# Near-attention scores issued among the last projection panels of a two-layer diffusion backbone

## The chip, the cores and the metric

The kernel runs on one core of one Trainium2 chip. It is one program: TensorE (PE, with its weight loads PEld), VectorE (DVE), ScalarE (ACT), GpSimd (POOL) and SyncE (SP, which mostly issues DMAs) each run a list of instructions in order, and semaphores make one list wait for another. The metric is the device time of the whole program in microseconds, as the median of several executions.

## The reference

The model is two transformer layers over 512 latent tokens (a grid 64 wide, 8 rows) and 256 context tokens, with a width of 1024. The change concerns the first layer's attention, and there the eight neighbourhood heads. Its core:

```python
def na_heads(q, k, v, qc, kc, vc, rel_bias, ctx_out):
    ...
    s_lat = jnp.einsum('bnqhd,bknmhd->bhnqkm', qr, k_blk).astype(jnp.float32) * scale
    s_lat = s_lat + col_bias[:, dr_idx].transpose(0, 2, 3, 1, 4)[None]
    s_lat = jnp.where(col_ok[:, :, None, :], s_lat, NEG_INF)...
    s_ctx = jnp.einsum('bnqhd,bchd->bhnqc', qr, kc).astype(jnp.float32) * scale
    p = jax.nn.softmax(jnp.concatenate([s_ctx, s_lat], axis=-1), axis=-1)
    return p_ctx @ vc + p_lat @ v_blk
    ...
def even_mixer(a_lat, a_ctx, ...):
    p_lat = a_lat @ w_in          # one projection for all head groups
    p_ctx = a_ctx @ w_in
    o_mla = mla_heads(...)
    o_na = na_heads(...)
    return concatenate([o_mla, o_na]) @ w_out
```

Each latent query sees the keys of 16 columns around it in all 8 rows, with a learned bias by distance, and all context keys, in one softmax. Context queries see the context keys alone. Behind the mixer comes a SwiGLU; the second layer has sliding-window attention.

## The kernel before

Everything is float32. A product of two float32 matrices is made of three matmuls of a high and a low part (`mm3`, lines 345, 347 and 348). Activations lie with features on the partitions and 768 tokens along the row: 512 latent ones and 256 context ones.

**The projection panels.** `projections()` walks over twelve panels of the input projection. A panel loads 128 output features of the weight, splits it, and makes two runs of 24 matmuls, 512 columns wide for the latent tokens and 256 for the context ones (`project`). It yields after every two of the eight steps over the width, so a panel has eight yields and the whole loop 96. The last four panels are the queries and keys of the third and fourth pair of near heads. Between the yields `bg` starts pieces of the conditioning vectors (`mod_tile`): products on VectorE (L239), products on GpSimd (L256) whose sums ScalarE makes (L257), and small sums on VectorE (L243, L259, L260).

**The near heads.** When the panels are through, `attend(na_jobs())` runs. Near heads come in four pairs. A pair has three jobs: context query tiles 4 and 5, latent query tiles 0 and 1, latent query tiles 2 and 3, each job for both heads of the pair. A job has a front half: for each query tile, scores on TensorE into one of three PSUM banks called `s` (`stacked_scores`, L755 and L756), then `take` on VectorE (L565), which adds the bias tile and the negated score and takes the row's minimum, then the exponential with its sum on ScalarE (L561). Its back half transposes the probabilities on TensorE (L509), copies them out of PSUM on VectorE or ScalarE (L500, L501), and multiplies them with the values (L555). `attend` keeps one job's lag: it works on a job's front and on the back of the one before in turns given by `PATTERN`, with side work (`step`) mixed in.

**Side work of the near heads.** `split_pair` makes the high and low parts of the third and fourth pair's queries (`put_q`, L721 and L722) and keys (`put_k`, L735 and L736); for the third pair the high part of the keys is cast on VectorE, and the halves are then copied across partitions by four DMAs. `latent_norms` normalizes the compressed latents (sums of squares L995, root L998, reciprocal L999, gains L975). `mix` copies values for mixed tiles on GpSimd (L1143).

**The bias tiles.** A head has two bias tiles of 128 x 768 (384 KB), one for query tiles 0 and 1, one for 2 and 3. All of them share two buffers, tag `nb`. `nb_tiles(h)` is called for one head at a time and issues both of its loads, so the buffers are taken in the order head 0 first half, head 0 second half, head 1 first half, head 1 second half.

**What sets the order.** The program is traced in the order in which Python runs it, and each instruction has a priority from its place there, which `shifted` moves. The scheduler then places the instructions on each engine by priority and by when their inputs are ready in its own timeline. `behind(a, b)` fixes that a comes after b on the same engine.

Of the kernel before, what the change touches and what calls it, by code (L numbers as in the profile page):

```python
# [2 lines left out]

# [9 lines left out]
ALU = mybir.AluOpType  # L13

P = 128
# [4 lines left out]
NT = NL + NX  # L20
# [9 lines left out]
LOWEST = -3.0e38  # L30
# [27 lines left out]
KC = (0, 1, 0)  # L58
# [12 lines left out]
LATE = ((0, 1, 3, 5, 7), ()), (0,) * 4 + (1, 2, 2, 2, 1, 2, 2, 2, 1, 2, 3, 2, 1, 2, 3, 2, 0, 0), ((2,), (2,)) + ((0, 2, 4, 6),) * 3  # L71
FIRST = 2000
STEPS = ((2, 3, 4, 4), 5, 3)
HALVES = (slice(0, 256), slice(256, 512))
# [25 lines left out]
def hybrid_kernel(ctx: ExitStack, tc, I, out):  # L100
# [33 lines left out]
    def dma(o, i, eng=None):  # L134
        return (eng or nc.sync).dma_start(f(o), f(i))
# [182 lines left out]
    def bg(n=1):  # L318

        for _ in range(n):  # L320
            next(mods, None)
# [241 lines left out]
    def take(p, c, s, bias, start, nm):  # L563

        V.tensor_tensor_reduce(out=p[:, c], in0=s, in1=bias, op0=ALU.add, op1=ALU.min, scale=-1.0, scalar=start,  # L565
                               accum_out=nm)

# [160 lines left out]

    def put_k(ks, copies=True, hi=None):


        def use(src, c):
            for side, (k1, k2) in enumerate(ks):
                r, x = slice(64 * side, 64 * side + 64), slice(64 - 64 * side, 128 - 64 * side)
                (hi or S.copy)(k1[r, c], src[r])  # L735
                V.tensor_tensor(k2[r, c], src[r], f(k1[r, c]), op=ALU.subtract)  # L736
# [293 lines left out]
    def split_pair(p):  # L1030
# [6 lines left out]
        yield  # L1037
        put_k(sets[p][1], KC[1], how[RK[p - 2]])(k, slice(0, NT))
        yield
# [94 lines left out]
    VX = []  # L1134
# [10 lines left out]
    def na_jobs():  # L1145
        for p in range(4):
# [8 lines left out]
            sums, mins = T("sm", [P, 6, 2]), T("sm", [P, 6, 2])  # L1155
            hs = []
            for s in range(2):
                t1, ks = sets[p]
                hs.append(Head(s, stacked_scores(t1[s], ks[s]), keys_of(VN[p], s, VX[p]), None, nb_tiles(2 * p + s), -LOWEST, sums, mins))
            yield from pair_jobs(hs, po, True, finish(po, sums, 6))  # L1160
# [656 lines left out]
```

## Time and profile before

| | us |
|---|---|
| median of three executions | 1577.79 (1577.0 to 1583.72) |
| the profiled execution | 1578.6 |
| its span, first to last instruction | 1576.6 |
| TensorE busy in it | 1530.6 |
| VectorE busy | 1174.0 |
| ScalarE busy | 794.5 |
| GpSimd busy | 276.0 |

The span in forty equal slices, each digit the busy share of a slice in tenths, and the TensorE clock that was granted:

```profile
PE   6999999999999999999999999999999999999998
PEld 4787778887998999999999998877889999899998
DVE  4885777685878587777858675889976778678685
ACT  4563677775465243242423334548856545454453
PEclk9999999999999999999999999999999999999999
```

One slice is 39.4 us. The panels end in the fifth, and the near heads fill the rest of it and the sixth and seventh. A row of a timeline gives start and duration in us, engine, line, operation, output and inputs by the program's names, shapes, and in brackets how long the engine sat idle before it and what ended that. A row of the busy view gives a stretch, its length, then the busy time of TensorE, its weight loads, VectorE, ScalarE and GpSimd with their instruction counts, the granted clock (1.00 is full), the share of the DMA engines and their rate.

### The profile page before, as it was taken

The numbers are of one execution on the slowest core, as the hardware profiler recorded it, in microseconds if no ns is written. First come the engines' busy times: TensorE is split into PE (matmuls) and PEld (weight loads), VectorE is DVE, ScalarE is ACT, GpSimd is POOL, SyncE is SP. The second block draws the span as 40 slices with busy tenths as digits, with TensorE's granted clock in tenths as the row PEclk, the third lists the DMA queues.
The fourth block names the chain that finished last, engine by engine and source line by source line (L and its number), as shares of the span: only waits on it lengthen the run. The fifth ranks groups of instructions, "written<-read, shape, count | busy, mean of one in ns | idle before, by whom it ended". The sixth has DMA issues, their size and how long they took to land.

```text
span 1576.6 us, 26539 instructions
## 1 busy us (share of the span) xinstructions
PE 1530.6 (97%) x10024; PEld 1375.8 (87%) x10024; DVE 1174.0 (74%) x2345; ACT 794.5 (50%) x1607; POOL 276.0 (18%) x302
## 2 busy tenths in 40 slices
PE   6999999999999999999999999999999999999998
PEld 4787778887998999999999998877889999899998
DVE  4885777685878587777858675889976778678685
ACT  4563677775465243242423334548856545454453
POOL 0144624320111101102111131470012000000001
PEclk9999999999999999999999999999999999999999
DMA  9644242004654444646466494110125123323222
GB/s 317 250 131 175 78 129 73 11 7 160 207 168 143 154 165 161 219 134 264 157 202 236 146 351 145 49 46 2 68 78 164 52 98 126 98 90 128 86 96 87
DMA packets 76463, 214.90 MB, mean 136 GB/s; under 512 B 9872, under 2 KB 16400, under 8 KB 76336
## 3 DMA queue, kind: packets, MB, share of 16 engines
q1 hardware_dynamic: 59216, 144.42, 27.6%
q0 software_dynamic: 15968, 67.24, 12.3%
q8 instruction: 78, 1.28, 0.3%
q10 hardware_dynamic: 1152, 1.57, 0.3%
q14 instruction: 49, 0.40, 0.1%
HBM read 186.97 MB, written 23.07 MB: 133 GB/s over the span
## 4 chain that ended last, share of the span: by engine, by line
PE 79%; DVE 9%; DMA 5%; ACT 3%; issue 2%; POOL 1%; SPq 0%; DVEq 0%; ACTq 0%; POOLq 0%
PE pss L1388 5%; PE pss L1387 5%; PE pss L1386 5%; PE pso L555 4%; PE pss L345 4%; PE psd L345 4%; PE pss L348 4%; PE pss L347 4%; PE psd L348 4%; PE psd L347 4%; PE pst L345 3%; PE pst L1388 3%; PE pst L1386 3%; PE pst L348 3%; PE pst L347 3%; PE pst L1387 3%
## 5 line engine op out<-in xcount | busy, mean ns | idle before, releaser
L334 ACT CAST wh<-wr 128x1024 fp32r<-128x1024 f32 (+2 forms) x148 | 115.5, 795 | 210.9 <-DMA wr<-in_w_dn_dram 42.1
L335 DVE TENSOR_TENSOR wl<-wr,wh 128x1024 fp32r<-128x1024 f32 (+2 forms) x145 | 133.9, 930 | 81.7 <-ACT wh L334 81.5
L561 ACT ACTIVATE p<-p,sm 128x512 f32<-128x512 f32 (+3 forms) x144 | 105.0, 730 | 29.0 <-DVE sm L565 27.2
L1386 PE MATMUL pss<-b,wh 128*128 128x384 f32 (+1 forms) x346 | 107.8, 312 | 0.6 <-ACT b L371 0.6
L1387 PE MATMUL pss<-b,wh 128*128 128x384 f32 (+1 forms) x346 | 108.0, 312 | 0.1
L1388 PE MATMUL pss<-b,wl 128*128 128x384 f32 (+1 forms) x346 | 107.2, 312 | 0.0
L347 PE MATMUL psd<-b,wh 128*128 128x512 f32 (+3 forms) x262 | 89.7, 343 | 0.0
L301 DVE CUSTOM_DVE_ANT_0 p<-rope,cond 128x1024 bf16<-128x1024 f32 x64 | 76.9, 1221 | 11.0 <-DMA rope<-in_mod_w_dram 10.8
L291 POOL DMA_DIRECT2D rope<-in_mod_w_dram x48 | 25.6, 533 | 318.7 <-DVE mod L301 306.0
L345 PE MATMUL psd<-b,wh 128*128 128x512 f32 (+3 forms) x222 | 80.0, 360 | 1.2 <-ACT b L474 0.9
L348 PE MATMUL psd<-b,wl 128*128 128x512 f32 (+3 forms) x222 | 78.8, 356 | 0.0
L555 PE MATMUL pso<-ph,b 128*64 128x256 f32 (+1 forms) x384 | 77.5, 361 | 0.4 <-DVE ph L500 0.2
L555 PE MATMUL pso<-pl,b 128*64 128x256 f32 (+1 forms) x384 | 77.2, 359 | 0.0
L1386 PE MATMUL pst<-b,wh 128*128 128x384 f32 (+1 forms) x226 | 70.8, 313 | 3.1 <-ACT p L1436 1.8
L1373 ACT CAST wh<-pl 128x512 fp32r<-128x512 f32 x78 | 44.9, 619 | 52.0 <-PE pss L1387 22.8
L1388 PE MATMUL pst<-b,wl 128*128 128x384 f32 (+1 forms) x226 | 70.7, 313 | 0.2 <-DVE wl L1374 0.2
L1387 PE MATMUL pst<-b,wh 128*128 128x384 f32 (+1 forms) x226 | 70.6, 312 | 0.0
L347 PE MATMUL pss<-b,wh 128*128 128x256 f32 (+3 forms) x216 | 69.3, 321 | 0.0
L1373 ACT CAST wh<-wr 128x1024 fp32r<-128x1024 f32 x39 | 41.0, 1051 | 54.4 <-PE pst L1387 14.7
L345 PE MATMUL pss<-st,wh 128*128 128x512 f32 (+2 forms) x198 | 67.2, 339 | 0.3 <-ACT wh L334 0.3
L348 PE MATMUL pss<-st,wl 128*128 128x512 f32 (+2 forms) x198 | 67.3, 340 | 0.1
L1386 PEld LDWEIGHTS pss<-b,wh 128*128 128x128 f32 x346 | 65.7, 190 | 1.1 <-ACT b L371 0.9
(624 smaller groups left out, 5387.4 us busy)
## 6 DMA issues: line engine op xcount, KB each, us to landing
wr<-in_w_gu_dram SPq DMA_DIRECT2D x88, 512.0 KB, 4.1
rope<-in_mod_w_dram POOLq DMA_DIRECT2D x48, 512.0 KB, 3.9
wr<-in_w_dn_dram SPq DMA_DIRECT2D x73, 256.0 KB, 2.9
wr<-in_w_out_dram SPq DMA_DIRECT2D x32, 512.0 KB, 4.2
p<-home POOLq DMA_DIRECT2D x40, 384.0 KB, 5.5
home<-p POOLq DMA_DIRECT2D x40, 384.0 KB, 5.4
wr<-in_w_in_dram SPq DMA_DIRECT2D x21, 512.0 KB, 3.8
nb<-in_nb_dram SPq DMA_DIRECT2D x16, 384.0 KB, 3.3
```

Of the source, the lines that this page charges most:

```text
L301: behind(V.tensor_tensor_reduce(out=T("p", [P, D], mybir.dt.bfloat16), in0=w, in1=cond[:, v, :], op0=ALU.mult, op1=ALU.add, scale=1.0, sca ...
L334: behind(S.copy(h, r), *after[:1])
L335: behind((G if eng else V).tensor_tensor(lo, r, f(h), op=ALU.subtract), *after[1:])
L345: ins = PE.matmul(o, wh[:, k], mh[:, c], start=first and k == 0, stop=False)
L347: PE.matmul(o, wh[:, k], ml[:, c], start=False, stop=False)
L348: PE.matmul(o, wl[:, k], mh[:, c], start=False, stop=last and k == n - 1)
L555: ins = PE.matmul(o[64 * i : 64 * i + 64, c], v(kt), t, start=n == 0, stop=n == len(moving[i]) - 1)
L561: S.activation(p[:, c], p[:, c], AF.Exp, bias=nm, scale=-1.0, accum_out=dn)
L1373: S.copy(h, t)
L1386: PE.matmul(o, wh, xh, start=first and k == 0, stop=False, skip_group_check=not first)
L1387: PE.matmul(o, wh, xl, start=False, stop=False, skip_group_check=not first)
L1388: PE.matmul(o, wl, xh, start=False, stop=k == 3, skip_group_check=not first)
```

## The change

It has three parts.

- `fronts()` takes the first two jobs of `na_jobs()` and runs their front halves (scores, `take`, exponentials) from inside the projection loop: a piece at each of the yields 82, 84, 86, 88, 90, 92 and 94, that is in the last two panels. `attend` then gets these jobs with an empty first step (`resumed`), and the others as before. What stands ahead of the first `yield` in `na_jobs` (the first side work, `mix`, the bias loads, `split_pair`'s start) is thereby traced earlier too.
- `nb_tiles(p)` is called for a pair, and issues the first halves of both heads, then the second halves.
- For the third pair, `split_pair` waits two more steps between queries and keys, and its first cast of the keys must stand behind the latest `take` that has been traced by then (`marks["take"]`).

```diff
+FRONTS = (82, 84, 86, 88, 90, 92, 94)
+QUIET = 2
...
-        V.tensor_tensor_reduce(out=p[:, c], in0=s, in1=bias, op0=ALU.add, op1=ALU.min, scale=-1.0, scalar=start,
-                               accum_out=nm)
+        marks["take"] = V.tensor_tensor_reduce(out=p[:, c], in0=s, in1=bias, op0=ALU.add, op1=ALU.min, scale=-1.0, scalar=start,
+                                               accum_out=nm)
...
-    def put_k(ks, copies=True, hi=None):
+    def put_k(ks, copies=True, hi=None, after=()):
...
-                (hi or S.copy)(k1[r, c], src[r])
+                behind((hi or S.copy)(k1[r, c], src[r]), *after)
...
-    def nb_tiles(h):
-        ts = [T("nb", [P, NT]) for i in range(2)]
+    def nb_tiles(p):
+        ts = {}
         for i in range(2):
-            dma(ts[i], I["nb"][h, i])
+            for s in range(2):
+                ts[s, i] = T("nb", [P, NT])
+                dma(ts[s, i], I["nb"][2 * p + s, i])
         cut = (slice(0, 512), slice(256, 768), slice(256, 768), slice(0, 512))
-        return lambda n: ts[n // 2][:, cut[n]]
+        return [lambda n, s=s: ts[s, n // 2][:, cut[n]] for s in range(2)]
...
-        put_k(sets[p][1], KC[1], how[RK[p - 2]])(k, slice(0, NT))
+        if p == 2:
+            for _ in range(QUIET):
+                yield
+        put_k(sets[p][1], KC[1], how[RK[p - 2]], after=(marks["take"],) if p == 2 else ())(k, slice(0, NT))
...
-    i = 0
+    def resumed(j):
+        yield False
+        yield from j
+
+    def fronts():
+        for _ in range(2):
+            early.append(next(jobs))
+            yield from iter(early[-1].__next__, False)
+
+    jobs, early, i = na_jobs(), [], 0
+    ahead = fronts()
     for _ in projections():
         i += 1
         bg(int(i * DBG) - int(i * DBG - DBG))
+        if i in FRONTS:
+            next(ahead, None)
+    for _ in ahead:
+        pass
     dense[0] = False
-    attend(na_jobs())
+    attend(chain((resumed(j) for j in early), jobs))
```

The lines of the changed file stand three to five further down: the scores L755 and L756 are L758 and L759 there, `take` L565 is L568, the transposes L509 are L512, the key split L735 and L736 is L738 and L739, DMAs of L135 are of L138.

What that does to the order is shown at three places. The first is TensorE at the end of the last panel. Before, the last two products of the panel's context run (`pst_1773`) are followed by the first context scores of both heads:

```order
L347 MATMUL pst_1773<-b_113,wh_1735 128x256
L348 MATMUL pst_1773<-b_112,wl_1736 128x256
L755 MATMUL pss_1833<-st_654,st_652 128x256
L756 MATMUL pss_1833<-st_655,st_652 128x256
L755 MATMUL pss_1843<-st_656,st_653 128x256
L756 MATMUL pss_1843<-st_657,st_653 128x256
```

In the changed kernel a near tile of the second head (`pss_1834`) stands between the latent run (`psd_1793`) and the context run of the same panel, and behind that run come the transposes of the first job:

```order
L350 MATMUL psd_1793<-b_113,wh_1789 128x512
L351 MATMUL psd_1793<-b_112,wl_1790 128x512
L758 MATMUL pss_1834<-st_656,st_653 128x192
L759 MATMUL pss_1834<-st_657,st_653 128x192
L758 MATMUL pss_1834<-st_656,st_653 128x64
L759 MATMUL pss_1834<-st_657,st_653 128x64
L758 MATMUL pss_1834<-st_656,st_653 128x256
L759 MATMUL pss_1834<-st_657,st_653 128x256
L348 MATMUL pst_1845<-b_98,wh_1789 128x256
...
L351 MATMUL pst_1845<-b_112,wl_1790 128x256
L512 MATMUL pst_1899<-ident_r_86,p_1693 128x128 x4
L512 MATMUL psd_1906<-ident_r_86,p_1715 128x128 x4
```

So the scores of the first two jobs, 28 matmuls, all stand ahead of the panel's end; the last of them are those shown.

The second place is VectorE, where the third pair's key split stood. Before, it lies among the last products of the conditioning and ahead of the first `take`; `b_1855` to `b_1857` are parts of the third pair's keys, `pl_1784` a conditioning weight:

```order
L735 CAST b_1855<-p_1563 64x768
L239 ISA p_1786,mod_293_1376<-pl_1784,cond_66,mod_293_1376 128x512
L239 ISA mod_293_1376 128x1
L736 TENSOR_TENSOR b_1856<-p_1563,b_1855 64x768
L735 CAST b_1857<-p_1563 64x768
L243 SCALAR_TENSOR_TENSOR mod_293_1376<-mod_293_1376,modb_89 128x1
L565 ISA p_1834,sm_1824<-pss_1833,zeros_95 128x256
```

In the changed kernel the same parts are `b_1891` to `b_1893`, and they stand among the takes of the first pair's last job (bias tile `nb_1690`), the fourth pair's key split (`st_2164`), and the second pair's first takes:

```order
L738 CAST b_1891<-p_1563 64x768
L739 TENSOR_TENSOR st_2164<-p_1786,st_2163 64x768
L568 ISA p_1994,sm_1683<-pss_1991,nb_1690 128x512
L568 ISA sm_1683 128x1
L568 ISA p_2009,sm_1999<-pss_2008,zeros_95 128x256
L568 ISA sm_1999 128x1
L503 COPY ph_1968<-pst_1963 128x512
L739 TENSOR_TENSOR b_1892<-p_1563,b_1891 64x768
L738 CAST b_1893<-p_1563 64x768
L568 ISA p_2033,sm_1999<-pss_2032,zeros_95 128x256
```

The split has moved from ahead of the near heads to behind the takes of two jobs and part of a third.

The third place is the queue of SyncE. The first two bias tiles are loaded long before in both programs. Before, the next ones are both halves of the first pair's second head (`nb_1829`, `nb_1830`), then the second pair's first head (`nb_2000`, `nb_2001`), with the copies of the third pair's keys (`b`) ahead of them:

```order
L135 DMA b_1855<-b_1855 64x768
L135 DMA b_1856<-b_1856 64x768
L135 DMA b_1857<-b_1857 64x768
L135 DMA b_1858<-b_1858 64x768
L135 DMA nb_1829<-in_nb_dram 128x768
L135 DMA nb_1830<-in_nb_dram 128x768
L135 DMA nb_2000<-in_nb_dram 128x768
L135 DMA st_2163<-st_2163 64x768
L135 DMA nb_2001<-in_nb_dram 128x768
```

In the changed kernel they are the second halves of both heads of the first pair (`nb_1688`, `nb_1690`), then the first halves of both heads of the second (`nb_2000`, `nb_2002`), with the key copies between and behind them:

```order
L138 DMA nb_1688<-in_nb_dram 128x768
L138 DMA nb_1690<-in_nb_dram 128x768
L138 DMA st_2163<-st_2163 64x768
L138 DMA nb_2000<-in_nb_dram 128x768
L138 DMA b_1891<-b_1891 64x768
L138 DMA st_2164<-st_2164 64x768
L138 DMA nb_2002<-in_nb_dram 128x768
L138 DMA st_2165<-st_2165 64x768
L138 DMA b_1892<-b_1892 64x768
L138 DMA b_1893<-b_1893 64x768
```

The bias loads keep their number and size; each is now issued when a first half has been used by its head, and the key copies stand behind two bias loads.

More of the change, by code (lines that the diff above doesn't have):

```diff
@@ L2 @@
 from contextlib import ExitStack, contextmanager
+from itertools import chain
 import numpy as np
@@ L1155, in na_jobs @@
             sums, mins = T("sm", [P, 6, 2]), T("sm", [P, 6, 2])
-            hs = []
+            hs, near = [], nb_tiles(p)
             for s in range(2):
                 t1, ks = sets[p]
-                hs.append(Head(s, stacked_scores(t1[s], ks[s]), keys_of(VN[p], s, VX[p]), None, nb_tiles(2 * p + s), -LOWEST, sums, mins))
+                hs.append(Head(s, stacked_scores(t1[s], ks[s]), keys_of(VN[p], s, VX[p]), None, near[s], -LOWEST, sums, mins))
             yield from pair_jobs(hs, po, True, finish(po, sums, 6))
```

## The prediction

> **What bounds the kernel now.** I read the page first, then the busy time by stretches around the place of the change, then the timelines of TensorE, VectorE and ScalarE inside those stretches, and last the answer on the bias tile.
>
> ```profile
> PE 1530.6 (97%) x10024; PEld 1375.8 (87%) x10024; DVE 1174.0 (74%) x2345; ACT 794.5 (50%) x1607; POOL 276.0 (18%) x302
> ```
>
> TensorE is busy for 1530.6 of 1576.6 us, so all that any change of order can win is in the other 46.0 us, and in stretches at a lower clock. The next view says where some of both lie: the last projection panels, then the near heads up to the last bias step of the second pair (211.02), then the rest of the near heads, then the heads behind them.
>
> ```profile
> core 0: us, PE busy (x) PEld busy (x) DVE busy (x) ACT busy (x) POOL busy (x), PEclk, DMA share, GB/s
> 159.15:175.83 16.68, 16.68 (x98) 14.77 (x97) 12.44 (x25) 7.52 (x18) 10.81 (x9) 1.00 0.04 14
> 175.83:211.02 35.19, 31.29 (x222) 26.18 (x220) 25.14 (x70) 27.88 (x66) 15.95 (x11) 0.90 0.46 128
> 197.50:211.02 13.52, 13.10 (x112) 11.61 (x110) 10.88 (x29) 11.16 (x25) 0.00 (x0) 1.00 0.53 146
> 211.02:257.40 46.38, 43.76 (x316) 35.09 (x315) 37.80 (x89) 35.22 (x85) 19.16 (x15) 0.96 0.31 94
> 257.40:355.00 97.60, 96.99 (x729) 78.92 (x729) 69.25 (x203) 72.09 (x165) 28.89 (x20) 1.00 0.09 24
> ```
>
> In the panels TensorE has no idle time (16.68 of 16.68), while ScalarE is busy for only 7.52 us. Behind them it idles for 35.19 - 31.29 = 3.90 us, and then for 2.62 us. From 257.40 on it is busy for 99%, so whatever arrives there earlier stays earlier. The clock column is 0.90 and 0.96; a finer grid shows why.
>
> ```profile
> 176.22:179.64 3.42, 2.24 (x13) 1.40 (x11) 3.33 (x8) 3.19 (x8) 3.22 (x4) 1.00 0.56 136
> 179.64:183.05 3.41, 3.00 (x14) 3.00 (x15) 1.75 (x8) 2.37 (x7) 3.25 (x3) 0.50 0.27 58
> 183.05:186.47 3.42, 3.42 (x17) 3.42 (x18) 0.25 (x1) 0.85 (x4) 3.34 (x3) 0.50 0.37 115
> 189.88:193.29 3.41, 1.99 (x14) 1.46 (x12) 0.96 (x3) 3.36 (x8) 2.84 (x2) 1.00 0.74 214
> 210.36:213.77 3.41, 1.57 (x9) 1.19 (x10) 3.41 (x9) 2.51 (x6) 0.65 (x1) 1.00 0.78 214
> 213.77:217.19 3.42, 3.42 (x15) 2.12 (x15) 2.93 (x8) 3.42 (x8) 3.34 (x4) 0.50 0.14 49
> ```
>
> Three stretches run at half clock, each set right behind a stretch in which TensorE was busy for 2.24 us or less (183.05 follows another slow one). That is 10.25 us at half speed, or 5.1 us of lost work. While TensorE crawls, VectorE is busy for 0.25 of 3.42 us: it waits for TensorE, not the other way round.
>
> ```profile
> 175.71 0.28 PE L348 MATMUL pst<-b,wl 128*128 128x256 f32 x1
> 180.05 0.53 PE L755 MATMUL pss<-st,st 128*128 128x192 f32 x1 [0.84 <-DVE sm L565]
> 193.50 0.39 PE L755 MATMUL pss<-st,st 128*128 128x256 f32 x1 [1.62 <-DVE sm L565]
> 213.44 0.79 PE L509 MATMUL psd<-ident_r,p 128*128 128x128 f32 x4 [1.54 <-DVE b L975]
> 186.22 0.69 DVE L500 COPY pl<-pst 128x512 f32<-128x512 f32 x1 [3.78 <-PE pst L509]
> 192.74 0.69 DVE L565 CUSTOM_DVE_ANT_0 wr<-pss,nb 128x512 f32<-128x512 f32 x1 [2.45 <-DMA nb<-in_nb_dram]
>   DVE wr L565: 3.5, 3
> DMA to landing us min/median/max: 2.9/3.1/4.0
> ```
>
> The first row is the last projection product. The next three are TensorE's waits: twice for a score bank that L565 on VectorE (add the bias, take the minimum) must empty. The last three rows say that this step itself waits 3.5 us in all for bias tiles, since of the four tiles of a pair the third is loaded only when a buffer comes free, with a landing time of about 3.1 us. So the stage is a **chain of latencies**: scores, L565, exponential, transposes, copies, with each engine between 71% and 89% busy.
>
> **The change, part by part.** Durations are those of the profiled execution, 1578.6 us long with a span of 1576.6; that is 0.8 us above the median of the runs, 1577.79, and I subtract that at the end.
>
> *Scores moved ahead.* The new order puts the scores of two jobs between the projection products: four context tiles and the first near query tile of both heads, sixteen matmuls 256 columns wide, and the second near query tile of both heads, two groups of six.
>
> ```profile
> 176.07 0.28 PE L755 MATMUL pss<-st,st 128*128 128x256 f32 x1
> 176.19 0.28 PE L756 MATMUL pss<-st,st 128*128 128x256 f32 x1
> 203.09 0.25 PE L755 MATMUL pss<-st,st 128*128 128x192 f32 x1
> 203.77 0.49 PE L509 MATMUL pst<-ident_r,p 128*128 128x128 f32 x3
> 164.82 1.14 DVE L260 SCALAR_TENSOR_TENSOR mod<-mod,modb 128x1 f32<-128x1 f32 x1
> ```
>
> Wide ones follow each other by 0.12 us: 16 x 0.12 = 1.9. A group of six runs from 203.09 to 203.77: 2 x 0.68 = 1.4. TensorE issues in order, so a score that needs a bank again stops the panel until L565 has run. The first L565 stands behind the L260 that ends here at 165.96, and with 0.34 of its own and the read of the sum it ends about 166.4; TensorE is back at that bank after 12 products of 0.23, 8 of 0.12 and two scores from 162.0, at about 165.9. I put 0.4 us down for it; the bounds are 0 and the 6 us of the slow rival below. The panels then end at 175.83 + 1.9 + 1.4 + 0.4 = **179.5**. Nothing of this is won yet: the same matmuls are missing behind it.
>
> *Work behind the panels.* What was between 175.83 and 211.02 is now this, for VectorE and ScalarE:
>
> ```profile
> 177.03 0.41 DVE L565 CUSTOM_DVE_ANT_0 p<-pss,zeros 128x256 f32<-128x256 f32 x1
> 177.37 0.41 DVE L565 CUSTOM_DVE_ANT_0 p<-pss,zeros 128x256 f32<-128x256 f32 x1
> 189.00 0.68 DVE L565 CUSTOM_DVE_ANT_0 p<-pss,nb 128x512 f32<-128x512 f32 x1
> 189.61 0.68 DVE L565 CUSTOM_DVE_ANT_0 p<-pss,nb 128x512 f32<-128x512 f32 x1
> 171.94 0.69 DVE L239 CUSTOM_DVE_ANT_0 p<-ph,cond 128x512 bf16<-128x512 f32 x1
> 174.35 0.73 DVE L239 CUSTOM_DVE_ANT_0 p<-pl,cond,mod 128x512 bf16<-128x512 f32 x1
> 173.88 0.55 DVE L735 CAST b<-p 64x768 fp32r<-64x768 f32 x1 [1.24 <-PE pst L348]
> 175.02 1.14 DVE L736 TENSOR_TENSOR b<-p,b 64x768 fp32r<-64x768 f32 x1
> 207.63 1.13 DVE L975 SCALAR_TENSOR_TENSOR b<-b,mla_gain,psd 128x512 f32<-128x512 f32 x2
> 176.44 1.28 ACT L561 ACT_TABLE_LOAD   x1
> 177.73 0.51 ACT L561 ACTIVATE p<-p,sm 128x256 f32<-128x256 f32 x1
> 182.47 0.72 ACT L561 ACTIVATE p<-p,sm 128x512 f32<-128x512 f32 x1 [0.64 <-DVE sm L565]
> ```
>
> VectorE loses four short L565 at 0.34 and four long ones at 0.61 (start to start): -3.8. It gains what stood in the panels and is now behind them: the last two products L239 (0.69 + 0.73) and the first half of the third pair's key split (0.55 + the 0.81 of L736 that lay before 175.83): +2.8. The two gains L975 and a reciprocal now come after the last bias step: -1.3. So 25.14 - 3.8 + 2.8 - 1.3 = **22.8 us**. ScalarE loses the table load and eight exponentials, 1.28 + 4 x 0.51 + 4 x 0.72 = 6.2: 27.88 - 6.2 = 21.7. In the panels they fit: ScalarE had 16.68 - 7.52 = 9.2 us free there, VectorE 4.2 and the 3.3 us by which the panels grow.
>
> How long 22.8 us of VectorE take is not in the trace of before; it depends on how well the chain is filled. Bounds from rows: 71% (25.14 of 35.19, as now) gives 32.1 us and an end at 211.6, a loss of 0.6; 100%, the row 210.36:213.77, gives 202.3, a win of 8.7. Nearest is the rest of the near heads without the front's stall: VectorE's 10.88 of 13.52 is 80%, its 37.80 of 46.38 is 81.5%, and ScalarE's 11.16 of 13.52, the busier engine there, is 82.5%. I take 82%: 27.8 us, an end at 207.3, **3.7 us won**.
>
> *Bias tiles by query half.* Both heads' first halves now come first, and the second halves are asked for when the first job is through. For the pairs from the second on, a load of 3.1 us has two L565 of the other head, a copy and a sum of squares in front of its use, some 3 us (four rows of 0.6 to 0.9), so most of the 3.5 us of waits are covered; were that cover gone, they would be back. About 2.7 of them lie before 211.02 and are inside the 82%. Behind it are 2.62 us of TensorE idle time and 1.7 lost at half clock; the wait for L975 is one of them, and the new order still runs six L975 in a row ahead of four transposes. Between 0 and 4.3 I take **1.3**, nearer to nothing.
>
> *Third pair's key split held.* The cast on VectorE may now not stand before the last step of the first pair's first near job. Behind it queue the subtraction and, on the DMA queue, four copies:
>
> ```profile
> 174.46 5.34 SPq L135 DMA_DIRECT2D b<-b  x4
> ```
>
> They now stand between bias loads instead of ahead of them. Issues there are short, and the third pair's scores, their only reader, come after the second pair's last scores, some 10 us later; that hides them. I cost them nothing beyond the 1.4 us already in the VectorE sum; with the cover gone, one landing of 3 us.
>
> **Sum:** 3.7 + 1.3 = 5.0 us. 1578.6 - 5.0 = 1573.6 for a profiled execution, **1572.8** as a median.
>
> The Trainium skill, page "TensorE: Matmul & The Clock Gate", section "Part 1: The HAM clock gate (the "warmup" mystery)", says that the clock falls to half after at least one idle window of about 3.4 us. No row here shows such an idle time: the longest near the slow stretches is 1.62 us, and that one was not followed by half clock. By the measured rows a thin stretch is enough, by the page's rule these waits would not be the cause; what follows then is the fourth rival.
>
> **The rivals.**
>
> 1. *Full recovery.* The chain fills as well as TensorE allows: 8.7 us less a little, and about 3 behind it: 11 us, 1566.8. For it: all three engines have room, and half clock itself caused VectorE's 3.78 us of waiting. Against it: near 100% on VectorE is shown only for 3.4 us at a time.
> 2. *The queue only moves.* The held split and the last two products fill VectorE where the scores used to, transposes wait for copies, and the rate stays at 71%: a loss of 0.6 and a little won behind, 1577.5. For it: three casts and four subtractions now stand among the copies. That the change does not do what it says belongs here too: the scores do stand among the panels, but exponentials that are late on ScalarE would leave the transposes waiting all the same.
> 3. *Slower: the panels stall.* Place: the five points among the last panels where a score waits for a bank. VectorE runs in order and three sums of products there wait for ScalarE, which waits for GpSimd:
>
> ```profile
> 171.67 0.16 DVE L259 TENSOR_TENSOR mod<-part,part 128x1 f32<-128x1 f32 x1 [2.02 <-ACT pl L257]
> ```
>
> Three such waits of 2.02 are 6.1 us of a TensorE that idles now for nothing, and two half-clock stretches behind them 3.4 more: 9.5 lost against 5.0 won, 1582.3. It decides from 5 us of stall on. Against it: between two uses of a bank there are mostly 2 us or more of products.
>
> 4. *Half clock stays.* If the two stretches at 179.64 do not come from the waits ahead of them, they stay, and 3.4 of the 5.0 us with them: 1576.2.
>
> **How the numbers follow.** The forecast, 1568.5 to 1575.5, gets 0.42; full recovery 0.20; the moved queue 0.20; half clock that stays 0.08, since three of three slow stretches follow a thin one; stalled panels 0.10. The range 1565.5 to 1578.5 takes in the forecast, most of the first rival, and the second and fourth; some 0.17 is left outside, mostly the slow rival. Half a per cent, about what a measurement of this kernel can tell from no change, is 7.9 us: faster means under 1569.9, which is rival 1 and a fifth of the forecast, 0.28; slower means over 1585.7, part of rival 3, 0.04; the rest is 0.68.
>
> **What would show it.** Right: the stretch behind the panels runs at a clock of 1.00, its first transposes follow the last projection product at once, L565's waits for the bias tile are under 1 us, and VectorE is some 82% busy up to the second pair's last bias step, which ends 27 to 29 us behind the panels. Wrong: TensorE idle for more than 1 us inside the last two panels; half clock again behind them; VectorE below 75%; or a wait of TensorE for L975 that has grown from 1.54 us. Should the time fall by 5 us with the stretch from 257.40 on also changed, the sum was right by accident.

## The result, and the profile after

The changed kernel is slower, not faster, by a quarter of one per cent: 1582.98 us median of 22 executions (1577.69 to 1590.5) against 1578.1 us of the kernel before in the same session (22 executions, 1574.53 to 1586.73). The ratio is 1.0025, 95% interval 1.0014 to 1.0036, so about 4 us. The prediction was 1572.8 us, in a range of 1565.5 to 1578.5; the result lies above the range.

The profiled execution took 1581.9 us with a span of 1579.5. From the page after:

```profile
PE 1529.5 (97%) x10024; PEld 1373.0 (87%) x10024; DVE 1181.2 (75%) x2345; ACT 795.0 (50%) x1607; POOL 277.5 (18%) x302
```

VectorE does the same 2345 instructions as before and is busy for 7.2 us more. That is the first hint of the cause. (Line numbers shift: L565 of before is L568, L736 is L739, L722 is L725, L239 is L242, L975 is L980, L988 is L993, L335 is L338, L509 is L512.)

TensorE's timeline after, at the end of the panels and at its longest wait there (start, duration, engine, line, operation, shapes, and in brackets the idle time ahead and what ended it):

```profile
180.10 0.29 PE L351 MATMUL pst<-b,wl 128*128 128x256 f32 x1
180.23 0.60 PE L512 MATMUL pst<-ident_r,p 128*128 128x128 f32 x4
...
192.35 0.58 PE L758 MATMUL pss<-st,st 128*128 128x256 f32 x1 [3.61 <-DVE sm L568]
```

The panels end at 180.39 and the first transposes follow at once, as the change means them to. Eight microseconds later, from 188.74 to 192.35, TensorE waits 3.61 us for one bias step on VectorE, longer than any wait there before (1.62). What VectorE did ahead of that step, and shortly after it:

```profile
187.30 0.67 DVE L503 COPY ph<-pst 128x512 f32<-128x512 f32 x1
187.89 1.31 DVE L738 CAST b<-p 64x768 fp32r<-64x768 f32 x1
189.13 2.55 DVE L739 TENSOR_TENSOR st<-p,st 64x768 fp32r<-64x768 f32 x1
191.61 0.67 DVE L568 CUSTOM_DVE_ANT_0 p<-pss,nb 128x512 f32<-128x512 f32 x1
...
193.17 2.08 DVE L739 TENSOR_TENSOR b<-p,b 64x768 fp32r<-64x768 f32 x1
195.28 1.72 DVE L738 CAST b<-p 64x768 fp32r<-64x768 f32 x1
...
199.62 0.96 DVE L739 TENSOR_TENSOR b<-p,b 64x768 fp32r<-64x768 f32 x1
```

The same subtraction L739 takes 0.96 us at 199.62, but 2.55 and 2.08 earlier; the cast L738, 0.55 us in the rows of before, takes 1.31 and 1.72. And GpSimd's timeline over the same time:

```profile
187.52 1.28 POOL L259 TENSOR_TENSOR pl<-pl,cond 128x512 f32<-128x512 f32 x1
188.88 2.00 POOL L725 TENSOR_TENSOR st<-p,st 64x768 fp32r<-64x768 f32 x1
190.95 5.63 POOL L993 TENSOR_TENSOR b<-b 128x768 f32<-128x768 f32 x3
```

Read the ends. L739 started at 189.13 while GpSimd was in L725, which ended at 188.88 + 2.00 = 190.88; L739 ended at 191.68, 0.80 us later, about its own undisturbed length. The cast at 187.89 ended at 189.20, 0.40 after the L259 of GpSimd (188.80). The cast at 195.28 ended at 197.00, 0.42 after the last L993 (196.58). None of these steps was slow; each **waited for the end of the instruction that GpSimd was in**, and the trace counts the wait as busy time. The bias steps and copies, which read PSUM, stay at 0.67 us. Of the 3.61 us gap these waits make 0.76 (cast) + 1.60 (subtraction) = 2.4; the other 1.2 us would be left without them, since the two steps, 0.55 and 0.95 us long alone, stand ahead of the bias step (an estimate from these rows).

The busy view, first from the end of the panels to the second pair's last bias step, then two stretches of the clock's grid (columns as in the prediction):

```profile
180.39:211.61 31.22, 26.19 (x180) 20.64 (x178) 27.96 (x56) 19.09 (x48) 15.72 (x9) 0.89 0.50 135
188.75:192.16 3.41, 0.00 (x0) 0.00 (x0) 3.41 (x3) 0.84 (x3) 3.25 (x3) 1.00 0.39 107
192.16:195.58 3.42, 3.23 (x18) 2.63 (x20) 3.39 (x7) 1.92 (x6) 3.42 (x3) 0.50 0.79 208
```

VectorE needs 27.96 us there where 22.8 were forecast. TensorE is idle through a whole stretch of 3.41 us, and the next runs at half clock.

### The profile page after: what moved, and what is told of

The parts are those of the page before. It is cut to its first block, busy times and chain, and to the rows that moved or that the text cites. A ratio compares the mean times of both kernels' runs of the same rounds, so it can differ in the third digit from the quotient of the medians.

```text
span 1579.5 us, 26527 instructions
## 1 busy us (share of the span) xinstructions
PE 1529.5 (97%) x10024; PEld 1373.0 (87%) x10024; DVE 1181.2 (75%) x2345; ACT 795.0 (50%) x1607; POOL 277.5 (18%) x302
## 4 chain that ended last, share of the span: by engine, by line
PE 70%; DVE 10%; DMA 4%; ACT 2%; issue 2%; POOL 1%; DVEq 0%; ACTq 0%; SPq 0%; POOLq 0%
PE pso L558 5%; PE pss L1410 4%; PE pss L1409 4%; PE pss L1408 4%; PE psd L348 3%; PE psd L351 3%; PE psd L350 3%; PE pss L348 3%; PE pst L1410 3%; PE pst L1408 3%; PE pss L351 3%; PE pst L1409 3%; PE pss L350 3%; DMA wr<-in_w_gu_dram 2%; PE pst L348 2%
## 5 line engine op out<-in xcount | busy, mean ns | idle before, releaser
L338 DVE TENSOR_TENSOR wl<-wr,wh 128x1024 fp32r<-128x1024 f32 (+2 forms) x145 | 133.9, 930 | 82.6 <-ACT wh L337 82.5
```

The costliest lines, as they stand in the source:

```text
L338: behind((G if eng else V).tensor_tensor(lo, r, f(h), op=ALU.subtract), *after[1:])
```

## The experiments

Theory A: the held key split meets GpSimd's work, waits for it, and holds up the bias step behind it. Theory B: moving the scores only moves the queue on VectorE. Theory C: the new order of the bias tiles costs the time. Later expectations call A the lock theory and B the queue theory. The table takes all runs together; the edits and expectations follow. "At 260" is how much later (+) or earlier the same TensorE instruction, counted from the first, starts at 260 us of the trace of before, less the same offset at 155 us, ahead of the change; so it leaves out what differs by chance ahead of the panels. "Idle" is 105 us less TensorE's busy time from 155 to 260 us. "Half" counts the stretches of 3.41 us at half clock in that window of the one profiled trace. "Lost" is the mean over all executions of (1 - granted clock) times span, and "rest" the mean span less that; the clock is given to 0.001, and both scatter by 2 to 3 us from one execution to the next, so that these means are good to some 0.6 us (0.2 for before). The ratios are to the kernel before in the same session, whose median was 1577.86 to 1579.79; between sessions, ratios are the better comparison.

| kernel | median us | ratio to before, 95% interval | at 260 | idle | half | lost | rest |
|---|---|---|---|---|---|---|---|
| before | 1578.9 (123 runs) | 1 | 0 | 6.5 | 3 | 11.8 | 1565.4 |
| changed | 1582.98 | 1.0025 [1.0014, 1.0036] | +0.84 | 8.7 | 2 | 14.5 | 1566.7 |
| changed, again | 1584.66 | 1.0035 [1.0021, 1.0048] | +1.79 | 10.0 | 2 | 14.9 | 1566.8 |
| hold off | 1577.99 | 0.9991 [0.9976, 1.0006] | -2.21 | 8.0 | 1 | 9.2 | 1567.1 |
| scores ahead alone | 1582.87 | 1.0019 [1.0004, 1.0033] | +4.01 | 10.4 | 4 | 13.2 | 1567.7 |
| tiles by half alone | 1587.75 | 1.0050 [1.0033, 1.0067] | +3.32 | 10.8 | 3 | 16.3 | 1569.7 |
| changed, squares on ScalarE | 1580.29 | 1.0004 [0.9988, 1.0019] | +0.09 | 8.9 | 3 | 13.0 | 1565.3 |
| changed, GpSimd cleared | 1581.19 | 1.0019 [1.0006, 1.0032] | -1.05 | 7.8 | 2 | 13.3 | 1565.8 |
| changed, split off VectorE | 1585.15 | 1.0055 [1.0037, 1.0072] | +6.59 | 9.9 | 6 | 19.3 | 1564.5 |
| V1: hold off, squares on ScalarE | 1575.34 | 0.9983 [0.9970, 0.9995] | -2.91 | 6.0 | 3 | 10.6 | 1563.3 |
| before, squares on ScalarE | 1579.17 | 1.0003 [0.9988, 1.0018] | +0.19 | 7.0 | 3 | 11.3 | 1566.0 |
| V1, third pair's low parts on VectorE | 1577.9 | 0.9989 [0.9975, 1.0004] | -3.29 | 6.3 | 3 | 14.2 | 1561.5 |
| **V2: V1, weights' low parts on VectorE** | **1574.88** | 0.9973 [0.9956, 0.9991] | -6.07 | 4.7 | 1 | 9.8 | 1563.1 |
| V2, again | 1575.44 | 0.9979 [0.9962, 0.9995] | -6.48 | 5.6 | 0 | 9.6 | 1563.4 |
| V2, all query low parts on VectorE | 1577.86 | 0.9994 [0.9981, 1.0007] | -2.87 | 4.2 | 4 | 15.0 | 1560.2 |
| V2, with the hold | 1577.83 | 1.0003 [0.9987, 1.0020] | -2.47 | 7.5 | 1 | 12.0 | 1564.8 |
| changed, GpSimd cleared, weights on VectorE | 1575.88 | 0.9985 [0.9968, 1.0002] | -3.29 | 5.3 | 2 | 11.0 | 1562.8 |

### The parts of the change

Hold off: `split_pair` as it was.

```diff
-        if p == 2:
-            for _ in range(QUIET):
-                yield
-        put_k(sets[p][1], KC[1], how[RK[p - 2]], after=(marks["take"],) if p == 2 else ())(k, slice(0, NT))
+        put_k(sets[p][1], KC[1], how[RK[p - 2]])(k, slice(0, NT))
```

> The changed kernel with the third pair's key split no longer held (scores ahead and bias tiles by half stay). Theory A (the held split runs on VectorE beside GpSimd's subtractions L725 and squares L993, is stretched, and the bias step behind it holds the score bank for 3.61 us): 2 to 6 us below the changed kernel, so 1577 to 1581, and no TensorE gap over 1.5 us between 185 and 200 us. Theory B (moving the scores ahead only moves the queue, whatever the split does): within 1.5 us of the changed kernel, about 1582, with a gap of 3 us somewhere else before 206 us.

It came out at 1577.99, 5.0 us below the changed kernel, and no wait between 185 and 200 us is as long as 3.61 (the longest are 1.83 and 1.37, so A's bound of 1.5 was a little too low). Against B: without the hold there was no wait of 3 us anywhere before 206. In the table the whole 5.0 us is in "lost" (9.2 against 14.5); "rest" did not fall. The waits for GpSimd are not gone, though; they fall on smaller steps. VectorE's timeline of this kernel:

```profile
193.86 1.43 DVE L262 TENSOR_TENSOR mod<-part,part 128x1 f32<-128x1 f32 x1
195.32 1.39 DVE L263 SCALAR_TENSOR_TENSOR mod<-mod,modb 128x1 f32<-128x1 f32 x1
```

and GpSimd's:

```profile
191.78 4.92 POOL L993 TENSOR_TENSOR b<-b 128x768 f32<-128x768 f32 x3
```

Two steps on one column, which take 0.16 us each in the changed kernel at 176.96 and 177.16, take 1.4 us beside the squares, and the second ends at 196.71, where GpSimd's run ends too (191.78 + 4.92 = 196.70).

Scores ahead alone: the hold off, and the bias tiles asked for head by head as before.

```diff
-        for i in range(2):
-            for s in range(2):
+        for s in range(2):
+            for i in range(2):
                 ts[s, i] = T("nb", [P, NT])
```

> Scores ahead alone: the bias tiles head by head as before, the key split not held. Theory A: 1576 to 1579, at most 1 us above the kernel before. Theory B: 1581 to 1583, as the changed kernel. Theory C (it is the order of the bias tiles that costs): as the kernel before or below it, while the tiles alone cost 3 us.

1582.87: A's expectation failed. The answer on the bias tile says what the scores ahead do with the old order of loads; first this kernel, then the changed one:

```profile
  DMA nb<-in_nb_dram: 5.7, 4
```

```profile
  DMA nb<-in_nb_dram: 1.4, 2
```

The bias steps wait 5.7 us for tiles instead of 3.5 before and 1.4 in the changed kernel. The scores ahead need the new order of tiles: with it (hold off) the time is 4.9 us lower. Theory C is out as the account of the 4 us, since this kernel has the old order and is as slow as the changed one.

Tiles by half alone: the changed kernel with the front generator and the hold taken out.

```diff
-    jobs, early, i = na_jobs(), [], 0
-    ahead = fronts()
+    i = 0
...
-        if i in FRONTS:
-            next(ahead, None)
...
-    attend(chain((resumed(j) for j in early), jobs))
+    attend(na_jobs())
```

> Bias tiles by query half alone: no scores ahead, no hold. Theories A and B: 1576 to 1578.5, the waits of the bias step for the tile shorter than 3.5 us in all. Theory C: 1580 to 1583.

1587.75, above every expectation, although the waits for tiles fell from 3.5 us to 0.2. Its VectorE timeline shows the same kind of wait at another place:

```profile
177.78 1.98 DVE L739 TENSOR_TENSOR b<-p,b 64x768 fp32r<-64x768 f32 x1
179.78 0.69 DVE L568 CUSTOM_DVE_ANT_0 p<-pss,nb 128x512 f32<-128x512 f32 x1
```

L739 stands beside an L725 of GpSimd, takes 1.98 us, and TensorE waits 1.63 us for the bias step behind it. The idle time in the window is 4.2 us more than before. Part of the loss lies elsewhere: two waits of 1.8 us near 374 and 400 us, where the order on ScalarE differs from before although no line there was changed; the scheduler had placed it anew. The rest of this miss stays open; tiles alone are slow, as C said, but by more than C said.

So the parts do not add up, in us against before: scores ahead alone +3, tiles alone +8, the two together -1, and with the hold +4.

### Whether GpSimd is the cause

Squares on ScalarE, with the hold:

```diff
-RK, RQ, RL, SQ = (2, 0), (0, 0), (0, 0), 1
+RK, RQ, RL, SQ = (2, 0), (0, 0), (0, 0), 0
```

> The changed kernel with the three squares of the latent norms on ScalarE and not on GpSimd. Theory A: the key split's steps beside them fall back from 1.7 to 2.6 us towards 0.95 (those beside L725 stay long), the 3.61 us gap shrinks by 1 us or more, and the time falls by 1 to 3 us, to 1580 to 1582. Theory B: the steps and the gap stay and the time is within 1 us of the changed kernel.

2.7 us below the changed kernel (3.3 by the ratios). The steps beside the squares fell to 0.94 and 0.56 us, as A said, but the gap stayed at 3.61: the two steps ahead of it meet L259 and L725, not the squares. A was right on the wait and wrong on which of them made the gap.

GpSimd cleared; this kernel leaves the low parts of the third and fourth pair's queries out of its result:

```diff
-RK, RQ, RL, SQ = (2, 0), (0, 0), (0, 0), 1
+RK, RQ, RL, SQ = (2, 0), (0, 0), (0, 0), 0
...
-        put_q(sets[p][0], None, how[RQ[p - 2]], (G, V)[RL[p - 2]].tensor_tensor)(q, slice(0, NT))
+        put_q(sets[p][0], None, how[RQ[p - 2]], lambda o, x, y, op: S.copy(o, x))(q, slice(0, NT))
```

> The changed kernel, hold included, without GpSimd's work beside the held split: the squares are on ScalarE, and the four subtractions L725 (low parts of the third and fourth pair's queries) are replaced by copies on ScalarE, so the output leaves those differences out. Lock theory (a VectorE step whose operands all lie in SBUF begins only when the instruction that GpSimd is in has ended; here that makes 6.6 us of waits between 182 and 197 us): L739 0.95 us and L738 0.55 each where no L259 runs, the 3.61 us gap below 1.5, and 3 to 6 us less than the changed kernel, 1577 to 1580. Queue theory (the split costs by standing ahead of the bias steps, locked or not): the gap stays above 2.5 us and the time above 1581.

This run shows the waits most directly. Its busy view from the end of the panels to the second pair's last bias step:

```profile
180.05:207.88 27.83, 25.62 (x180) 20.59 (x178) 22.74 (x56) 25.46 (x57) 3.71 (x3) 0.88 0.52 153
```

The same 56 instructions of VectorE, in a slightly different order, take 22.74 us instead of 27.96, in 27.83 us instead of 31.22. Its VectorE timeline at the place of the gap:

```profile
186.96 0.67 DVE L568 CUSTOM_DVE_ANT_0 p<-pss,nb 128x512 f32<-128x512 f32 x1
...
187.91 0.55 DVE L738 CAST b<-p 64x768 fp32r<-64x768 f32 x1
...
189.32 0.94 DVE L739 TENSOR_TENSOR st<-p,st 64x768 fp32r<-64x768 f32 x1
190.19 0.67 DVE L568 CUSTOM_DVE_ANT_0 p<-pss,nb 128x512 f32<-128x512 f32 x1
...
220.46 1.79 DVE L1123 CAST st<-b 32x768 fp32r<-32x768 f32 x1
222.28 0.69 DVE L503 COPY pl<-pst 128x512 f32<-128x512 f32 x1
```

The split runs at full speed with the hold in place, and the longest wait of TensorE before 208 us is 0.91. Not all of the vanished gap is the lock, though: here the long bias step at 186.96 stands ahead of the cast, where in the changed kernel it stands behind the cast and a subtraction, so that most of the 1.2 us of queue named above went too. The time fell only to 1581.19, 1.2 us above the expected range, and by the ratios only 0.9 us below the changed kernel, less than the intervals can tell from nothing. The last two rows say why: behind the second pair another GpSimd run, the low part of a weight,

```profile
219.49 2.35 POOL L338 TENSOR_TENSOR wl<-wr,wh 128x1024 fp32r<-128x1024 f32 x1 [1.49 <-ACT wh L337]
```

ends at 221.84, the cast beside it at 222.25, and TensorE waits 1.78 us for the copy behind the cast.

Split off VectorE: casts on ScalarE, subtractions on GpSimd.

```diff
-    def put_k(ks, copies=True, hi=None, after=()):
+    def put_k(ks, copies=True, hi=None, after=(), lo=None):
...
-                V.tensor_tensor(k2[r, c], src[r], f(k1[r, c]), op=ALU.subtract)
+                (lo or V.tensor_tensor)(k2[r, c], src[r], f(k1[r, c]), op=ALU.subtract)
...
-        put_k(sets[p][1], KC[1], how[RK[p - 2]], after=(marks["take"],) if p == 2 else ())(k, slice(0, NT))
+        put_k(sets[p][1], KC[1], S.copy, (marks["take"],) if p == 2 else (), G.tensor_tensor if p == 2 else None)(k, slice(0, NT))
```

> The changed kernel with the held split taken off VectorE: its two casts on ScalarE, its two subtractions on GpSimd. Lock theory and queue theory both expect the 3.61 us gap gone and 2 to 5 us less than the changed kernel, 1578 to 1581, unless GpSimd, some 3.7 us longer, locks VectorE's other steps in turn: then the gap only moves and the time stays at 1582 to 1584.

2.2 us above the changed kernel, where 2 to 5 us below were expected, or 1582 to 1584 should the gap move. It moved, and the time is above that too: the wait of 3.61 us shrank to 1.52, and others grew behind it. GpSimd's timeline, then TensorE's:

```profile
195.52 4.32 POOL L993 TENSOR_TENSOR b<-b 128x768 f32<-128x768 f32 x3
```

```profile
217.66 0.61 PE L512 MATMUL psd<-ident_r,p 128*128 128x128 f32 x2 [3.19 <-DVE b L980]
```

The squares now end at 199.84 instead of 196.58, but that is not what delays the gains L980: the root L1003 that they need runs at 209.65, earlier than in the changed kernel (212.45). On VectorE the gains stand behind an L375 that started at 214.80, when a cast of ScalarE had ended, and took 1.39 us beside an L338 of GpSimd (0.95 alone). Six stretches at half clock make it the variant that loses most to the clock (19.3 us), and by "rest" (1564.5) it is below before: what it is slower by is clock.

The changed kernel, a second time:

> The changed kernel once more, for a second trace. If the 1.20 us wait for a weight load at 124.88 us, ahead of all that the change touches, is chance, it is not there again; the 3.61 us gap and the VectorE steps of 2.55, 2.08 and 1.72 us are there again within 0.1 us; stretches at half clock lie elsewhere, and their number may differ. If the wait at 124.88 is part of the change's cost, it is there again.

The wait at 124.88 was chance; TensorE's timeline in the two traces, first then again:

```profile
124.88 0.62 PE L213 MATMUL pst<-ph,cond_col 128*32 128x256 f32 x4 [1.20 <-DMA ph<-in_mod_wp_dram]
```

```profile
124.93 0.60 PE L213 MATMUL pst<-ph,cond_col 128*32 128x256 f32 x4
...
192.06 0.58 PE L758 MATMUL pss<-st,st 128*128 128x256 f32 x1 [3.60 <-DVE sm L568]
```

The gap and VectorE's steps (2.55, 2.08, 1.71) came back within 0.01 us. The stretches at half clock did not: at 192.16 and 202.40 in one trace, two in a row from 190.84 in the other.

### What the gain needs

V1, hold off and squares on ScalarE (both edits above):

> Scores ahead and bias tiles by half, no hold, and the squares on ScalarE. Lock theory: the small steps L262 and L263, 1.43 and 1.39 us behind GpSimd's squares with the hold off, fall to 0.16, and the time is 1 to 3 us below hold off, 1575 to 1577. Queue theory: within 1 us of hold off, 1577 to 1579.

1575.34, as A said, and a little below before by its interval; L262 and L263 take 0.16 us each. By the ratios it is 1.3 us below hold off, so the time alone does not rule B out. The control, the kernel before with its squares on ScalarE:

> The kernel before with the squares on ScalarE alone: no scores ahead, old bias order. If the gain of the last variant (scores ahead, tiles by half, no hold, squares on ScalarE: 0.9983 of before) came from the squares alone, this is within 1 us of it, about 2.5 to 3 us below the kernel before. If scores ahead and tiles are worth the predicted 3 to 5 us once VectorE is not locked, this is at most 1.5 us below the kernel before: in its trace the squares hold up VectorE only once, by 0.2 us.

1.0003: the squares alone win nothing. The gain comes from the scores ahead and the tiles, once VectorE's steps meet less of GpSimd.

V1 with the third pair's low parts on VectorE:

```diff
-RK, RQ, RL, SQ = (2, 0), (0, 0), (0, 0), 0
+RK, RQ, RL, SQ = (2, 0), (0, 0), (1, 0), 0
```

> Scores ahead, tiles by half, no hold, squares on ScalarE, and the third pair's two low parts on VectorE (0.95 us each) in place of GpSimd (2.1 and 2.4 us). Lock theory: the two L242 behind the panels, 1.50 and 2.18 us, fall to 0.7 and at most 1.9; VectorE's sum changes by -0.4 to +1; the time stays within 1.5 us of the last variant. Queue theory (only what stands on VectorE counts): 2 us more.

2.6 us above V1 (0.9 by the ratios, within A's bound), but its first L242 grew to 2.28 us, since the fourth pair's L725 took the place of the third's beside it. "Rest" fell by 1.8 us, and "lost" rose by 3.6. It tells the theories apart by neither number.

V2, which is V1 with the weights' low parts on VectorE:

```diff
-        wu["kv"] = load_w(I["w_ukv"], 2, 512, G)
-        w = load_w(I["w_qr"], 2, 256, G)
-        wu["qn"] = load_w(I["w_qn"], 2, 512, G)
+        wu["kv"] = load_w(I["w_ukv"], 2, 512)
+        w = load_w(I["w_qr"], 2, 256)
+        wu["qn"] = load_w(I["w_qn"], 2, 512)
```

> Scores ahead, tiles by half, no hold, squares on ScalarE, and the low parts of the three latent-head weights on VectorE (1.22, 0.65, 1.22 us) in place of GpSimd's 2.4, 1.3, 2.4. Lock theory: the VectorE step L1120 of 1.51 us and the first L375 of 1.17 fall to 0.55 and 0.95, and the 2.24 us gap of TensorE near 217 us shrinks below 1.3; the time falls by 0 to 2 us. Queue theory: 3 us more on VectorE make it slower by 1 to 3 us.

0.5 us less than V1 (1.6 by the ratios, within the noise), with three more steps on VectorE: L1120 fell from 1.51 to 0.55 us and the 2.24 us gap to 1.24, as A said; B's 1 to 3 us more did not come. This is the fastest version, 0.9973 of before.

V2 with all four low parts of the queries on VectorE as well (`RL` (1, 1)):

> All of it together: scores ahead, tiles by half, no hold, squares on ScalarE, all four low parts and the three weights' low parts on VectorE, so that GpSimd does little there but L259 and the copies of the mixed values. Lock theory: hardly a VectorE step over its undisturbed time between 180 and 225 us, VectorE's own sum about 7 us more; time within 2 us of the last variant, either side. Queue theory: 4 us or more above it.

1577.86, 3.0 us above V2, between the two expectations. TensorE idles least of all here, but four stretches in a row run at half clock:

```profile
185.34:188.75 3.41, 2.07 (x15) 1.79 (x15) 3.35 (x8) 3.39 (x6) 1.28 (x1) 1.00 0.20 42
188.75:192.17 3.42, 2.66 (x10) 2.16 (x11) 3.42 (x9) 3.07 (x10) 0.00 (x0) 0.50 0.66 183
192.17:195.58 3.41, 3.41 (x19) 3.41 (x17) 3.32 (x9) 1.75 (x6) 0.00 (x0) 0.50 0.74 192
195.58:198.99 3.41, 3.41 (x20) 2.81 (x21) 1.23 (x6) 3.27 (x8) 1.58 (x4) 0.50 0.15 33
198.99:202.41 3.42, 3.42 (x19) 2.29 (x16) 0.73 (x4) 2.11 (x4) 0.00 (x0) 0.50 0.00 0
```

Over all its runs "rest" is 5.1 us below before and "lost" 3.1 above: the clock took most of what the order had won.

The last three were run together: V2 with the hold put back, the changed kernel with GpSimd cleared and the weights on VectorE (the edits above put together), and V2 again.

> The changed kernel, hold included, with the squares on ScalarE and the three latent-head weights' low parts on VectorE. It differs from the fastest variant only in the hold. If the hold costs only because VectorE's held steps meet GpSimd's subtractions L725, the 3.61 us gap is still there (the step of 2.55 us beside L725 is untouched) and the time is 2 to 5 us above the fastest variant, 1577 to 1580. If the hold as such is harmless, within 1 us of it.

> The changed kernel, hold included, with all of GpSimd's work between 180 and 225 us out of the way but L259 and the copies of the mixed values: squares on ScalarE, the four subtractions L725 replaced by ScalarE copies (the output leaves those differences out), the three weights' low parts on VectorE. Lock theory: VectorE 22.5 to 23.5 us busy behind the panels up to the second pair's last bias step, which ends at 207 to 208.5; no step of VectorE over 1 us by waiting for L338 behind it; the trace at 260 us is 2.5 to 5 us ahead of the kernel before, and the idle part of the predicted 5.0 us is there. Queue theory: the trace at 260 us is within 1.5 us of the kernel before, as in the variant with L338 on GpSimd (1.05 ahead).

> The fastest variant once more, beside a variant that differs from it only in the hold. If its 0.9973 was no draw of the half-clock stretches: 0.996 to 0.999 of the kernel before, the trace 4 us or more ahead at 260 us.

The hold costs 2.4 us (1577.83 against 1575.44; 4.0 in the traces at 260). It does so for the most part by the meeting, as VectorE's timeline in V2 with the hold shows:

```profile
189.85 2.55 DVE L739 TENSOR_TENSOR st<-p,st 64x768 fp32r<-64x768 f32 x1
192.33 0.67 DVE L568 CUSTOM_DVE_ANT_0 p<-pss,nb 128x512 f32<-128x512 f32 x1
```

TensorE waits 3.60 us for that bias step once more. With the hold in place and GpSimd out of the way behind the panels and behind the second pair (the second kernel), VectorE is again busy for 22.78 us, the second pair's last bias step ends at 208.52, in a trace that is 1.01 us late ahead of the panels, and the trace is 3.29 us ahead at 260, where the hold with L338 on GpSimd had 1.05. So what was given back behind the second pair was the same kind of wait. The time of this second kernel, 1575.88, is some 2.4 us below before (0.9985, interval up to 1.0002), about half of the 5.0 us that were forecast. V2 stayed at 0.9979 of before.

## Why the prediction was wrong, point by point

**The panels: right.** Forecast were an end at 179.5 and 0.4 us of stall. The forecast counted the panels' end as 0.12 us after the start of the last product, which is 180.22 here, in a trace that runs 0.64 us late for the chance wait ahead of them: 179.58, with 0.13 us of stall. The rival of the stalled panels did not come.

**VectorE's 22.8 us behind the panels: the step that failed.** The sum counted the right instructions, and took for their durations there what the rows showed at their old place; it had no term for GpSimd. The 28.0 us of the changed kernel are 21.4 of work and 6.6 of waits for GpSimd: 1.5 us on L242, 0.5 on L246, 1.9 on the two casts and 2.7 on two of the subtractions. With GpSimd cleared 1.3 us of these waits were left, and the forecast came out: 22.74 us of VectorE, 82% of 27.83 us, an end at 207.88 less the 0.28 us by which that trace is late, 207.6 against the forecast 207.3. Some of that closeness is luck: the 25.14 us that the sum started from hold 0.9 us of such waits themselves (0.5 of them in the L736 at 177.83 of before), and the stretch was forecast at a clock of 1.00 and ran at 0.88. In the changed kernel that step ends at 211.61 - 0.64 = 210.97, where before ended: the 3.7 us were not won.

**The key split, costed at nothing: wrong.** The prediction asked what queued behind it on VectorE and on the DMA queue, not what ran beside it on GpSimd. Before, the first half of the split stood in the panels; the hold moved it to where GpSimd makes the low parts and the squares. It costs 2.4 us in the cleanest pair of runs and 5.0 in the changed kernel, there all of it in "lost".

**Bias tiles: right in kind.** The waits for tiles fell from 3.5 to 1.4 us, and with scores ahead the new order is worth 4.9 us. The 1.3 us forecast behind 211.02 were not seen: from the second pair's last bias step (0.1 us ahead of before) to 260 us (0.84 behind) the changed kernel loses 1 us. The run with GpSimd cleared, with and without L338, shows 2.2 us of such waits there; in the changed kernel itself they were not taken apart.

**Half clock: wrong in what was expected to vanish.** The two stretches at 179.64 went, but one came right behind the 3.61 us gap, at 192.16, and one at 202.40, behind a stretch with TensorE busy for 2.84 of 3.41 us. Over all runs the changed kernel loses 14.5 us to the lower clock and before 11.8, so of its 4 us some 2.7 are clock and 1.3 the rest. Where in the program the extra loss falls is not shown: in the traced window the changed kernel has two slow stretches and before has three. The Trainium skill, page "TensorE: Matmul & The Clock Gate", section "Part 1: The HAM clock gate (the "warmup" mystery)", asks for an idle window; the stretch 188.75:192.16 is one (0.00 of 3.41 us busy) and half clock follows, but in V2 with all query low parts on VectorE half clock follows a stretch with 2.07 us busy, so here an idle window is not needed. Nor is a thin one enough, as the prediction took it: its own view has 189.88:193.29 with 1.99 us busy, and no half clock behind it.

**The rivals.** The stalled panels came nearest by number (1582.3), which is luck, since that stall was 0.13 us. "The queue only moves" came nearest by reason, at 1577.5 and with the split as its cause, yet its price was a fill rate of 71%; VectorE was 90% full, of work and waits. It has a share, the 1.2 us of the gap that are queue. No rival had an engine waiting for another engine's instruction with no data between them. The rows of before held it: the L260 quoted in the prediction took 1.14 us on one column, where the step beside it, L259, took 0.16, and GpSimd's timeline of before shows what it waited for:

```profile
164.66 1.29 POOL L256 TENSOR_TENSOR pl<-pl,cond 128x512 f32<-128x512 f32 x1 [0.69 <-DVE mod L239]
```

It ends at 165.95, L260 at 165.96. The prediction used that row as a duration.

## What to carry to other kernels

Where instructions of one shape have very different durations, the longer ones may contain a wait: lay their ends beside the ends of the other engines' instructions before using any of them in a sum. When a step moves, ask what runs beside it at the new place on the engines that it shares nothing with by data, not only what queues behind it. And a gain of a few microseconds in a stage where stretches at half clock come and go should be measured as idle time and clock apart, since the one can pay for the other.

## What the runs showed of the hardware

A VectorE step with two inputs in SBUF, or a cast from SBUF to SBUF, waited for the end of the instruction that GpSimd was already in: steps of 0.15 to 0.95 us took up to 2.55, and ended 0.0 to 0.8 us after GpSimd's instruction, by about their own length or less. It goes the other way too: GpSimd's three squares take 4.32 us alone in the trace of before (at 184.28) and 5.63 in the changed kernel, among the split's steps. Steps that read PSUM kept their 0.67 us beside the same GpSimd work. The Trainium skill, page "SBUF — State Buffer", section "Who interferes with whom", says so: VectorE with two SBUF inputs, or in a two-port mode as casts can be, shares a port with GpSimd, and whoever is second fully blocks. The traces agree. The same build's stretches at half clock lay at different places in two traces, over all traces they came one to four in a row, and much of the spread of one kernel's runs is this: of 123 runs of before, 1572.95 to 1587.93 us, the 15 with a mean clock of 0.990 had a mean span of 1580.8 us, the 23 at 0.994 one of 1574.8.
